# Ten sums and remainders go from VectorE to GpSimd and two come back; token sums and weight splits are issued at other places

## The chip, the cores and the metric

One Trainium2 chip, of which the kernel uses one core. The metric is the device time of one execution in microseconds, the median of the runs. Five engines work side by side, each through its own queue in order, and wait for one another by semaphores: TensorE (PE; its weight loads are PEld), VectorE (DVE), ScalarE (ACT), GpSimd (POOL) and SyncE (SP), which here only issues transfers.

## The reference

One encoder block over 1024 tokens of width 1024, float32, cut to its steps:

```python
h = rms_norm(x, norm1_g)
a, gate, q, k, v = split(h @ w_in)
conv_out = conformer_conv(a, gate, ...)            # gated, 31 taps in depth, norm, silu
attn_out = neighbourhood_attention(q, k, v, rpb)   # 8 heads, 8 x 16 windows
x = x + concat([conv_out, attn_out]) @ w_out
h = rms_norm(x, norm2_g)
x = x + (silu(h @ w_gate) * (h @ w_up)) @ w_down   # width 2816 in between
```

## The kernel before

Every product is made from split operands: a float32 matrix becomes a high part (`hi`, a cast by ScalarE) and a remainder (`lo`, the matrix less its high part, a subtraction by VectorE or GpSimd), and `mac` (L115 to L117) issues three matmuls, hi by hi, hi by lo and lo by hi. The helper `split` (L107 cast, L111 subtraction) takes the engine of the subtraction as an argument.

The feed-forward part works on the transposed state `xT[0..7]` (eight blocks of 128 rows by 1024 tokens) and on pairs i = 0 to 21 of column blocks of the gate and up weights. For each pair the two by two block product (halves of the rows, halves of the tokens) is made with seven products instead of eight, named m1 to m7 as in Strassen's and Winograd's scheme. This needs sums on both sides. On the side of the tokens: S1 to S4 and A22, made in place in `xT` by VectorE (`left`, sums on L1189), each of four blocks k = 0 to 3, with their casts and remainders (L111, or L1196 where the cast was issued apart). On the side of the weights: sums n = 1 to 4 for each pair (`t_sums`, L1024, tile `ts`, or `tqa` for pairs 0 and 1), and the splits of the operands for m1 to m7 (`prep`; tiles `t0m4` and the like, `tqb` and `tqc` for m1 and m2 of pairs 0 and 1, 2 and 3). The results go to the PSUM tiles A (m1, m2), D (m7, m4) and B (m6, m5, m3), and are read out by `evac` and `gate2`: `g` on L1283, L1287 and L1288, `u` on L1274, D on L1259, `g` on L1263. From pair 4 on, m1 and m2 are themselves made from seven smaller products (`part`, tiles `q40m1`, `q41m1`, `q42m1`); for these `tok_sum(m, n)` makes half-width sums of `xT` blocks (L1101, tiles `qtm`) and `prep_part` sums and splits of weights (`qs`, `qa` to `qd`).

Before the feed-forward part stands the output projection (`proj`, PSUM tiles `pj`, weights `wo`, split when `take()` is called), with the residual sum `resid` (L870), which reads `pj`, writes `xT` and frees the PSUM bank for the next `pj`. Then the squares of `xT` are summed (L980) for the second norm, which scales `xT` (`norm2`, L997, with the row `rw` in PSUM).

Nothing schedules the program: each engine's order is the order in which the code issues. The products are issued in the order of the list `products`; behind product number n the entries of the table `after[n]` are issued, then the splits that are due (`prep`). TensorE's order of products around the change is: m1 of pairs 0 and 1, m2 of both, the same for pairs 2 and 3, then m7, m4, m6, m5, m3 for pairs 0 and 1 in turn, then pair 2.

Of the kernel before, what the change touches and what calls it, by code (L numbers as in the profile page):

```python
# [9 lines left out]
OP = mybir.AluOpType  # L10
# [60 lines left out]
def build(ctx, tc, a):  # L71
    nc = tc.nc
    pe, act, dve, pool = nc.tensor, nc.scalar, nc.vector, nc.gpsimd
# [8 lines left out]
    def G(name, dt=F32):  # L82
        return T("G", [P, 1024], 21, name, dt)
# [4 lines left out]
    def H(name, dt=F32):  # L88
        return T("H", [P, 4096], 7, name, dt)
# [16 lines left out]
    def split(hi, lo, src, sub=(pool,)):  # L106
        act.copy(hi, src)  # L107
        n = src.shape[-1] // len(sub)
        for i, eng in enumerate(sub):
            sl = slice(i * n, (i + 1) * n)  # L110
            eng.tensor_tensor(*[w[..., sl] for w in (lo, src, hi.bitcast(F32))], OP.subtract)  # L111
# [7 lines left out]
    def lr(w):  # L119
        return w[:, :512], w[:, 512:]  # L120
# [19 lines left out]
    def issue():  # L140
        if pos[0] < len(chunks):
            src, name, _, _ = chunks[pos[0]]
            if pos[0] not in raws:
                raws[pos[0]] = R(name + "r")
            d = raws[pos[0]]
            if len(src.shape) == 3:
                d = d.rearrange("p (k m) -> p k m", k=src.shape[1])
            sl = slice(512 if name == "wk0" else 0, None)
            nc.sync.dma_start(d[:, sl], src[:, sl])
            pos[0] += 1  # L150

    def take(n=1, ahead=True):
        for _ in range(n):
            i = pos[1]
            while pos[0] <= i:
                issue()
            _, _, dst, sub = chunks[i]
            hi, lo = dst()
            split(hi, lo, raws.pop(i), sub)
            pos[1] += 1  # L160
            if ahead and pos[0] < i + 4:
                issue()
# [650 lines left out]
    def proj(m, h, ks, sel=None, every=1):  # L813
        out = cols(acc[m, h], sel)
        for n, k in enumerate(ks):
            r = [cols(w[:, k % 4], sel) for w in (cm if k < 4 else at)[h]]
            mac(out, [w[:, m % 4 * P:m % 4 * P + P] for w in wo[m // 4, k]], r, k == 4 and sel != INNER, k == 3)
            if n % every == every - 1:
                weave()
# [48 lines left out]
    def resid(m, h):  # L868
        w = xT[m][:, h * 512:(h + 1) * 512]
        dve.tensor_tensor(w, acc[m, h], w, OP.add)  # L870
        nc.sync.dma_start(xd[m][:, h * 512:(h + 1) * 512], w)
# [86 lines left out]
    for k in CONV:  # L958
        for m in range(4):
            proj(m, 0, (k,), None, 1 + (m + 1) % 2)  # L960
            if (k, m) == (3, 0):
                resid(0, 0)
        if k in (1, 2):
            take()
    for m in range(4, 8):
        load_xT(m)
    for m in range(1, 3):
# [31 lines left out]
    HK, QF = KB // 2, FB // 2  # L999
    raw_gu, top, tsum = {}, {}, {}  # L1000

    def load_gu(i, j):
        if i < FB:
            raw_gu[i, j] = R(f"gu{i}{j}")
            nc.sync.dma_start(raw_gu[i, j], a["gu"][ms[i], j])
# [3 lines left out]
    def tq_slot(name, q, dt=F32):  # L1009
        if name not in tqs:  # L1010
            tqs[name] = H(name, dt)
        return tqs[name][:, q * 1024:(q + 1) * 1024]

    def t_sums(i, ns):
        (b11, b21), (b12, b22) = lr(raw_gu[i, 0]), lr(raw_gu[i, 1])
        for n in ns:
            if n in (1, 3):
                if i > 1:
                    tsum[i, n // 2] = G(f"ts{i}{n}")
                else:  # L1020
                    tsum[i, n // 2] = tq_slot("tqa", 2 * i + n // 2)
            o = lr(tsum[i, (n - 1) // 2])[(n - 1) % 2]
            l, r = ((b12, b11), (b22, lr(tsum[i, 0])[0]), (b22, b12), (b21, lr(tsum[i, 0])[1]))[n - 1]
            dve.tensor_tensor(o, l, r, OP.subtract)  # L1024


    ORDER = ("m1", "m6", "m7", "m2", "m5", "m4", "m3")
# [65 lines left out]
    def tok_sum(m, n):  # L1093
        g, c = TOK_AT[n]
        if (m, g) not in tok_raw:
            tok_raw[m, g] = G(f"qt{m}{g}").rearrange("p (c k s) -> p c k s", c=2, s=256)
        for k in range(2):
            x11, x12, x21, x22 = [xT[2 * q + k + HK * (m == "m2")][:, e:e + 256] for q in range(2) for e in (0, 256)]
            s1, s2 = [tok_raw[m, TOK_AT[w][0]][:, TOK_AT[w][1], k] if (m, TOK_AT[w][0]) in tok_raw else None for w in (1, 2)]
            l, r = {1: (x12, x11), 3: (x22, x12), 2: (x22, s1), 4: (x21, s2)}[n]  # L1100
            dve.tensor_tensor(tok_raw[m, g][:, c, k], l, r, OP.subtract)  # L1101
# [49 lines left out]
    def prep(n=1, upto=None):  # L1151
        while tasks and (n > 0 if upto is None else tasks[0][0] <= upto):
            n -= 1
            job = tasks.pop(0)[1]
            if len(job) == 3:
                prep_part(*job)
                continue
            i, p = job
            if i > 1 and p in ("m6", "m7"):
                t_sums(i, (1, 2) if p == "m6" else (3, 4))  # L1160
            b = {"m1": (0, 0), "m2": (0, 1), "m3": (1, 1)}.get(p)
            m = {"m5": 0, "m6": 1, "m7": 2, "m4": 3}.get(p)
            src = lr(raw_gu[i, b[0]])[b[1]] if b else lr(tsum[i, m // 2])[m % 2]
            if i < 4 and p in ("m1", "m2"):
                top[i, p] = lr(tq_slot(("tqb", "tqc")[i // 2], i % 2 + 2 * (p == "m2"), F32R))
            else:
                top[i, p] = lr(G(f"t{i}{p}", F32R))
            split(*top[i, p], src, (dve,) if i < 2 else (pool,))
            if p == ("m7" if i in (2, 3) or parted(i, "m2") else "m2"):
                load_gu(i + 2, 0)  # L1170
            if p == "m3":
                load_gu(i + 2, 1)
# [5 lines left out]
    def block(r, k):  # L1178
        return xT[k % HK + HK * (r[1] == "2")][:, 512 * (r[0] == "2"):512 * (r[0] == "2") + 512]

    def left(n, k, what, sub=dve):
        if n not in sop:
            q = H(n, F32R).rearrange("p (w k s) -> p w k s", w=2, s=512)
            sop[n] = [[q[:, h, i] for i in range(HK)] for h in range(2)]
        o, l, r, op = {"S3": ("21", "11", "21", OP.subtract), "A22": ("22", "22", "22", None),
                       "S2": ("22", "22", "21", OP.subtract), "S1": ("21", "22", "11", OP.add),
                       "S4": ("22", "12", "22", OP.subtract)}[n]
        if op is not None and "sum" in what:
            dve.tensor_tensor(block(o, k), block(l, k), block(r, k), op)  # L1189
        hi, lo = sop[n][0][k], sop[n][1][k]  # L1190
        if "split" in what:
            split(hi, lo, block(o, k), (sub,))
        if "cast" in what:
            act.copy(hi, block(o, k))
        if what == "sub":
            sub.tensor_tensor(lo, block(o, k), hi.bitcast(F32), OP.subtract)  # L1196

    def lefts(n, sub=(dve,) * 4, first=None, upto=HK):
        for k in range(HK + 1):
            if k < HK:  # L1200
                first(k) if first else left(n, k, "sum")
            if 0 < k <= upto:
                left(n, k - 1, "split", sub[k - 1])

    def h2_one(k):
        norm2(k, 0)
# [6 lines left out]
    for m in range(4):  # L1213
        square(m, 0)
    beside = {(1, 1): [lambda: token_sums(0)], (1, 3): [lambda: token_rows(0)],
              (0, 1): [lambda: t_sums(0, (1, 2))], (0, 3): [lambda: t_sums(0, (3, 4))],
              (2, 1): [lambda: t_sums(1, (1, 2))], (3, 1): [lambda: t_sums(1, (3, 4))]}
    for kb, at_ in enumerate(((2, 0), (2, 3), (2, 6), (3, 1), (3, 4), (3, 7), (4, 3), (4, 7))):
        beside.setdefault(at_, []).append(lambda kb=kb: h2_one(kb))
# [162 lines left out]
    def prep_items(n):  # L1382
        for _ in range(n):
# [8 lines left out]
             6: lambda: [left("S1", k, "sum cast") for k in range(HK)],  # L1392
             7: lambda: left("S1", 0, "sub"),
             8: lambda: [left("S1", k, "sub") for k in (1, 2)],
             9: lambda: (left("S1", 3, "sub"), prep(), [tok_sum("m1", w) for w in (1, 3)]),
             10: lambda: ([tok_sum("m1", w) for w in (2, 4)], prep(), [left("S4", k, "sum cast") for k in range(HK)]),
             11: lambda: [left("S4", k, "sub") for k in (0, 1)],
             12: lambda: ([left("S4", k, "sub") for k in (2, 3)], prep()),
             18: lambda: [tok_sum("m2", w) for w in (1, 3)],
             19: lambda: [tok_sum("m2", w) for w in (2, 4)]}  # L1400
    prep(4)
# [46 lines left out]
    def quarter(w, o, t):  # L1448
        return w[:, o + t * 512:o + t * 512 + 512]
# [32 lines left out]
    for s, p in enumerate(SEQ):  # L1482
        for k in range(QF - 2):
            n = s * QF + k
# [23 lines left out]
    for half in range(2):  # L1508
# [4 lines left out]
        w = quarter(om["u"], 0, 3)[:, part_]  # L1513
# [17 lines left out]
```

## Time and profile before

| | |
|---|---|
| median of 3 runs | 1035.74 us (1035.32 to 1035.88) |
| profiled execution | 1035.18 us |
| its span | 1033.5 us |
| busy share of the span | PE 99%, PEld 83%, DVE 76%, ACT 46%, POOL 42% |
| granted TensorE clock | 1.0 throughout |
| transfers | 152.53 MB, mean 148 GB/s |

How to read it: the profile is one execution, and every share is an average over stages with different limits. Matmuls overlap, so that TensorE's busy share says little about short losses; these are read from the starts of successive matmuls. The chain that ended last gives 93% to PE and 5% to DVE; in the timeline of that chain the DVE part lies mostly between 415 and 475 us, where the first products of the feed-forward part are made. Names in profile rows leave out buffer numbers, so `S` may be any of S1 to S4, and `D<-A` is a product of A22 into D.

### The profile page before, as it was taken

The page shows a single profiled execution, that of the slowest core. Times are in us where ns is not written, and L with a number is a line of the kernel's source. Part 1 is how long each engine was busy: PE and PEld are TensorE (multiplying, and loading weights), DVE is VectorE, ACT ScalarE, POOL GpSimd, SP SyncE. Part 2 cuts the span into 40 slices and gives each one's busy share as a digit, 9 for nine tenths or more (in the row PEclk, how much of TensorE's full clock was granted, in tenths as well). Part 3 has the DMA queues.
Part 4 walks back from the last instruction along what each step waited for, and adds up shares of the span by engine and source line. Part 5 has one row for each costly group of instructions (what it writes and reads, how often), then busy time and mean ns, then how long its engine had stood idle before and what let it go on. Part 6 is the DMA issues. An engine that isn't in the chain of part 4 may idle for free.

```text
span 1033.5 us, 15158 instructions
## 1 busy us (share of the span) xinstructions
PE 1024.3 (99%) x5334; PEld 853.8 (83%) x5334; DVE 782.3 (76%) x1234; ACT 478.7 (46%) x1045; POOL 436.0 (42%) x345
## 2 busy tenths in 40 slices
PE   9999999999999999999999999999999999999998
PEld 7888888877787788877888888888888888888887
DVE  5788997896755376998787787787787767758874
ACT  7565348836866345523334334343342443433432
POOL 1036764524641345047776667567566200003210
PEclk9999999999999999999999999999999999999999
DMA  9426781337403621122434424434441696633631
GB/s 347 165 79 201 225 255 53 122 115 234 124 22 122 235 92 41 47 107 89 156 119 157 139 96 153 153 101 145 144 143 71 222 365 238 224 102 123 214 122 42
DMA packets 75084, 152.53 MB, mean 148 GB/s; under 512 B 13824, under 2 KB 22784, under 8 KB 74368
## 3 DMA queue, kind: packets, MB, share of 16 engines
q1 hardware_dynamic: 72992, 148.21, 42.5%
q10 hardware_dynamic: 2016, 3.36, 0.9%
q8 instruction: 42, 0.69, 0.3%
q14 instruction: 34, 0.28, 0.1%
HBM read 112.38 MB, written 44.76 MB: 152 GB/s over the span
## 4 chain that ended last, share of the span: by engine, by line
PE 93%; DVE 5%; ACT 1%; issue 1%; DMA 0%; ACTq 0%; DVEq 0%
PE B L115 5%; PE B L116 5%; PE B L117 5%; PE z L115 4%; PE z L117 4%; PE z L116 4%; PE D L115 3%; PE D L116 3%; PE D L117 3%; PE gl L117 3%; PE gl L116 3%; PE gl L115 3%; PE pj L115 3%; PE pj L116 3%; PE pj L117 3%; PE p L720 2%
## 5 line engine op out<-in xcount | busy, mean ns | idle before, releaser
L363 DVE SCALAR_TENSOR_TENSOR cv<-u,par,cv 128x1009 f32<-128x1009 f32 (+14 forms) x92 | 117.4, 1277 | 2.3
L389 POOL TENSOR_TENSOR pa<-pa,pr 128x1022 f32<-128x1022 f32 (+5 forms) x24 | 58.0, 2417 | 48.7 <-ACT pr L388 36.1
L107 ACT CAST op<-sr 128x512 fp32r<-128x512 f32 x77 | 47.7, 619 | 57.7 <-PE B2d L117 26.7
L1474 POOL TENSOR_TENSOR ou<-ou,resm 128x512 f32<-128x512 f32 x8 | 12.0, 1506 | 139.8 <-DVE ou L1465 126.1
L111 DVE TENSOR_TENSOR op<-sr,op 128x512 fp32r<-128x512 f32 x77 | 57.6, 748 | 16.5 <-ACT op L107 16.4
L709 POOL TENSOR_SCALAR e<-e,rs 128x288 f32<-128x288 f32 (+1 forms) x64 | 33.9, 545 | 41.8 <-DVE rs L707 40.1
L1024 DVE TENSOR_TENSOR ts<-gu,ts 128x512 f32<-128x512 f32 x40 | 46.3, 1158 | 0.7
L107 ACT CAST op<-wd 128x512 fp32r<-128x512 f32 x54 | 33.4, 619 | 28.5 <-DVE wd L1370 18.0
L698 ACT ACTIVATE e<-e,mx 128x288 f32<-128x288 f32 (+1 forms) x64 | 36.5, 572 | 18.8 <-DVE mx L693 16.9
L111 DVE TENSOR_TENSOR op<-wd,op 128x512 fp32r<-128x512 f32 x54 | 39.8, 738 | 1.7 <-ACT op L107 0.6
L693 DVE CUSTOM_DVE_ANT_0 e<-s,tab 128x288 f32<-128x288 f32 (+1 forms) x64 | 28.7, 503 | 13.6 <-PE s L680 13.6
L980 POOL TENSOR_TENSOR sq<-sq,sq 128x512 f32<-128x512 f32 x12 | 17.1, 1423 | 51.6 <-ACT sq L976 51.4
L1283 DVE TENSOR_TENSOR g<-D,g 128x512 f32<-128x512 f32 x22 | 15.2, 690 | 23.4 <-PE D L117 23.4
L416 ACT ACTIVATE sq<-z,r 128x64 f32<-128x64 f32 x96 | 28.3, 329 | 5.2 <-PE z L117 5.2
L1260 ACT ACTIVATE D<-D 128x512 f32<-128x512 f32 x22 | 12.8, 582 | 32.6 <-DVE D L1259 32.6
L388 ACT ACTIVATE pr<-u,par 128x1022 f32<-128x1022 f32 (+5 forms) x24 | 27.0, 1138 | 1.6 <-ACT vs L446 1.2
L720 PEld LDWEIGHTS p<-ident,e 128*96 128x96 f32 (+1 forms) x192 | 20.5, 133 | 6.8 <-POOL e L709 6.3
L115 PE MATMUL B2d<-op 128*128 128x512 f32 x66 | 25.8, 391 | 0.0
L117 PE MATMUL B2d<-op 128*128 128x512 f32 x66 | 25.7, 389 | 0.0
L116 PE MATMUL B2d<-op 128*128 128x512 f32 x66 | 25.7, 389 | 0.0
L739 PE MATMUL o<-e,vw 96*64 96x128 f32 (+1 forms) x384 | 24.7, 277 | 0.0
L720 PE MATMUL p<-ident,e 128*96 128x128 f32 (+1 forms) x192 | 24.4, 276 | 0.0
(1454 smaller groups left out, 3734.5 us busy)
## 6 DMA issues: line engine op xcount, KB each, us to landing
gu<-in_gu SPq DMA_DIRECT2D x44, 512.0 KB
sr<-sd SPq DMA_DIRECT2D x77, 256.0 KB
sd<-sd SPq DMA_DIRECT2D x22, 512.0 KB
wd<-in_wd SPq DMA_DIRECT2D x36, 256.0 KB
sd<-g SPq DMA_DIRECT2D x33, 256.0 KB
x<-in_x SPq DMA_DIRECT2D x8, 512.0 KB
xT<-in_xp SPq DMA_DIRECT2D x8, 512.0 KB
xd<-xT SPq DMA_DIRECT2D x16, 256.0 KB
```

Source lines behind the costliest of these rows:

```text
L107: act.copy(hi, src)
L111: eng.tensor_tensor(*[w[..., sl] for w in (lo, src, hi.bitcast(F32))], OP.subtract)
L115: pe.matmul(acc, lh, rh, start=start, stop=False, skip_group_check=True)
L116: pe.matmul(acc, lh, rl, start=False, stop=False, skip_group_check=True)
L117: pe.matmul(acc, ll, rh, start=False, stop=stop, skip_group_check=True)
L363: dve.scalar_tensor_tensor(acc[:, o], uc[:, i], dwk[:, c, t:t + 1], acc[:, o], OP.mult, OP.add)
L389: pool.tensor_tensor(pa[:, o], pa[:, o], pr[:, o], OP.add)
L693: dve.tensor_tensor_reduce(out=es[i][:, hh], in0=s[hh], in1=tab[rh, cb][2 * hp + hh], scale=-1.0, scalar=3.0e38, op0=OP.add, op1=OP.min, a ...
L698: act.activation(e, e, AF.Exp, bias=mx.pop((i, hh)), scale=-1.0, accum_out=sums[i][:, hh:hh + 1])
L709: pool.tensor_scalar(es[i][:, hh], es[i][:, hh], rs[:, hh:hh + 1], 1.0, op0=OP.mult, op1=OP.mult)
L720: pe.transpose(pt[:m, g * P:(g + 1) * P], es[i][:, hh, g * m:(g + 1) * m], ident)
L1024: dve.tensor_tensor(o, l, r, OP.subtract)
```

## The change

Ten subtractions named in a set `ON_POOL` are issued on GpSimd instead of VectorE: the remainders of S3 (k = 2, 3), A22 (k = 1) and S4 (k = 3), the weight sums n = 2 and 4 of pair 3, and the remainders of the weight operands m4 and m5 of pair 0 and m4 and m6 of pair 1. Two, the remainders of m3 and m7 of pair 3 (`ON_DVE`), go the other way. The split of the weights wo16, issued by the second of two `take()` calls, moves behind the residual sum of block 0. Of the token sums of m1, each two half-width subtractions, n = 2 moves one product earlier, n = 3 three later and n = 4 five later.

```diff
             proj(m, 0, (k,), None, 1 + (m + 1) % 2)
             if (k, m) == (3, 0):
                 resid(0, 0)
-        if k in (1, 2):
-            take()
+            if (k, m) in ((1, 3), (3, 0)):
+                take()
...
+    ON_POOL = {("S3", 2), ("S3", 3), ("A22", 1), ("S4", 3), (3, 2), (3, 4),
+               (0, "m4"), (0, "m5"), (1, "m4"), (1, "m6")}
+    ON_DVE = {(3, "m3"), (3, "m7")}
...
-            dve.tensor_tensor(o, l, r, OP.subtract)
+            (pool if (i, n) in ON_POOL else dve).tensor_tensor(o, l, r, OP.subtract)
...
-            split(*top[i, p], src, (dve,) if i < 2 else (pool,))
+            on_dve = (i < 2 and (i, p) not in ON_POOL) or (i, p) in ON_DVE
+            split(*top[i, p], src, (dve,) if on_dve else (pool,))
...
-    def left(n, k, what, sub=dve):
+    def left(n, k, what):
+        sub = pool if (n, k) in ON_POOL else dve
...
-             9: lambda: (left("S1", 3, "sub"), prep(), [tok_sum("m1", w) for w in (1, 3)]),
-             10: lambda: ([tok_sum("m1", w) for w in (2, 4)], prep(), [left("S4", k, "sum cast") for k in range(HK)]),
+             9: lambda: (left("S1", 3, "sub"), prep(), [tok_sum("m1", w) for w in (1, 2)]),
+             10: lambda: (prep(), [left("S4", k, "sum cast") for k in range(HK)]),
              11: lambda: [left("S4", k, "sub") for k in (0, 1)],
-             12: lambda: ([left("S4", k, "sub") for k in (2, 3)], prep()),
+             12: lambda: ([left("S4", k, "sub") for k in (2, 3)], prep(), tok_sum("m1", 3)),
+             15: lambda: tok_sum("m1", 4),
```

The orders of TensorE, ScalarE and SyncE are the same in both programs; those of VectorE and GpSimd differ in the places named. VectorE at the end of the output projection, where the residual sum of block 0 (L870, `xT0`) and the split of wo16 stand; first the program before, then the one after:

```order
L111 TENSOR_TENSOR cm1_3173<-z12_3503,cm1_3173 128x512
L111 TENSOR_TENSOR wo14_3480<-wo16r_3266,wo14_3480 128x1024
L870 TENSOR_TENSOR xT0_3416<-pj00_3088,xT0_3416 128x512
L111 TENSOR_TENSOR cm1_3173<-z13_3521,cm1_3173 128x512
L111 TENSOR_TENSOR wo10l_3544<-wo10r_3268,wo10h_3543 128x1024
```

```order
L111 TENSOR_TENSOR cm1_3173<-z12_3503,cm1_3173 128x512
L870 TENSOR_TENSOR xT0_3416<-pj00_3088,xT0_3416 128x512
L111 TENSOR_TENSOR wo14_3480<-wo16r_3266,wo14_3480 128x1024
L111 TENSOR_TENSOR cm1_3173<-z13_3521,cm1_3173 128x512
L111 TENSOR_TENSOR wo10l_3544<-wo10r_3268,wo10h_3543 128x1024
```

The two rows of `xT0` and `wo16r` have changed places (the tile `wo14` holds wo16's parts too).

VectorE between the sums of S3 and of S2, where the norms (L997) of blocks 4 to 7 and the remainders of S3 and A22 stand; before, then after:

```order
L1189 TENSOR_TENSOR xT3_3422<-xT3_3422 128x512
L111 TENSOR_TENSOR S3_4054<-xT2_3420,S3_4054 128x512
L111 TENSOR_TENSOR S3_4054<-xT3_3422,S3_4054 128x512
L997 SCALAR_TENSOR_TENSOR xT4_3535<-xT4_3535,par_73,rw1_4042 128x512
L997 SCALAR_TENSOR_TENSOR xT5_3537<-xT5_3537,par_73,rw1_4042 128x512
L111 TENSOR_TENSOR A22_4112<-xT4_3535,A22_4112 128x512
L997 SCALAR_TENSOR_TENSOR xT6_3539<-xT6_3539,par_73,rw1_4042 128x512
L111 TENSOR_TENSOR A22_4112<-xT5_3537,A22_4112 128x512
L997 SCALAR_TENSOR_TENSOR xT7_3541<-xT7_3541,par_73,rw1_4042 128x512
L111 TENSOR_TENSOR A22_4112<-xT6_3539,A22_4112 128x512
```

```order
L1195 TENSOR_TENSOR xT3_3422<-xT3_3422 128x512
L997 SCALAR_TENSOR_TENSOR xT4_3535<-xT4_3535,par_73,rw1_4042 128x512
L997 SCALAR_TENSOR_TENSOR xT5_3537<-xT5_3537,par_73,rw1_4042 128x512
L111 TENSOR_TENSOR A22_4112<-xT4_3535,A22_4112 128x512
L997 SCALAR_TENSOR_TENSOR xT6_3539<-xT6_3539,par_73,rw1_4042 128x512
L997 SCALAR_TENSOR_TENSOR xT7_3541<-xT7_3541,par_73,rw1_4042 128x512
L111 TENSOR_TENSOR A22_4112<-xT6_3539,A22_4112 128x512
```

S3's last two remainders and A22's second are gone from VectorE; they stand on GpSimd behind the `tqc` splits.

GpSimd between the split of `qb4m1` and that of `qc4m1`, which TensorE's parts `q41m1` and `q42m1` use (`ts31` and `ts33` hold the weight sums of pair 3, `qT3m1` a token sum); before, then after:

```order
L111 TENSOR_TENSOR qb4m1_4456<-qs4m1_4451,qb4m1_4456 128x512
L111 TENSOR_TENSOR t3m6_4462<-ts31_4459,t3m6_4462 128x512
L111 TENSOR_TENSOR qT3m1_4465<-qtm10_4225,qT3m1_4465 128x512
L111 TENSOR_TENSOR t3m7_4485<-ts33_4482,t3m7_4485 128x512
L111 TENSOR_TENSOR qc4m1_4521<-qs4m1_4451,qc4m1_4521 128x512
```

```order
L111 TENSOR_TENSOR qb4m1_4456<-qs4m1_4451,qb4m1_4456 128x512
L1028 TENSOR_TENSOR ts31_4459<-gu31_4246,ts31_4459 128x512
L111 TENSOR_TENSOR t3m6_4462<-ts31_4459,t3m6_4462 128x512
L111 TENSOR_TENSOR qT3m1_4465<-qtm10_4225,qT3m1_4465 128x512
L1028 TENSOR_TENSOR ts33_4482<-gu30_3802,ts31_4459 128x512
L111 TENSOR_TENSOR qc4m1_4521<-qs4m1_4451,qc4m1_4521 128x512
```

Two sums have come in, and the split of `t3m7` has gone to VectorE, where it stands behind the sum n = 3.

More of the change, by code (lines that the diff above doesn't have):

```diff
@@ L1196, in left, with lefts @@
             sub.tensor_tensor(lo, block(o, k), hi.bitcast(F32), OP.subtract)
-    def lefts(n, sub=(dve,) * 4, first=None, upto=HK):
+    def lefts(n, first=None, upto=HK):
         for k in range(HK + 1):
@@ L1202, in lefts @@
             if 0 < k <= upto:
-                left(n, k - 1, "split", sub[k - 1])
+                left(n, k - 1, "split")
     def h2_one(k):
```

## The prediction

> **What bounds the kernel now.** I read the page first, then the list of who waited for whom on TensorE, then the timeline of TensorE around each of these waits, then the timelines of VectorE (DVE), ScalarE (ACT) and GpSimd (POOL) over the same stretch. The page and one row of the table by stage:
>
> ```profile
> span 1033.5 us, 15158 instructions
> ...
> PE 1024.3 (99%) x5334; PEld 853.8 (83%) x5334; DVE 782.3 (76%) x1234; ACT 478.7 (46%) x1045; POOL 436.0 (42%) x345
> ```
>
> ```profile
> 430.00:440.00 10.00, 10.00 (x45) 8.25 (x45) 10.00 (x21) 3.18 (x6) 0.00 (x0) 1.00 0.45 150
> ```
>
> TensorE is idle for 1033.5 - 1024.3 = 9.2 us in all, so nothing off TensorE can bring more than some 1%. But in the stretch of the first products VectorE is the full engine: from 430 to 440 us it is busy 10.00 of 10.00 us, ScalarE 3.18, GpSimd 0.00. What a late VectorE costs there shows in TensorE's timeline, at five places (start, duration, and in brackets the idle time and who ended it):
>
> ```profile
> 337.51 0.40 PE L117 MATMUL pj<-cm,wo02l 128*128 128x512 f32 x1
> 338.96 0.50 PE L115 MATMUL pj<-at,wo 128*128 128x512 f32 x1 [1.05 <-DVE xT L870]
> ...
> 428.73 0.39 PE L116 MATMUL D<-S,t1m 128*128 128x512 f32 x1
> 428.95 0.39 PE L117 MATMUL D<-S,t1m 128*128 128x512 f32 x1
> 429.78 0.50 PE L115 MATMUL D<-A,t0m 128*128 128x512 f32 x1 [0.43 <-DVE g L1283]
> ...
> 443.29 0.39 PE L117 MATMUL B<-S,t0m 128*128 128x512 f32 x1
> 444.13 0.50 PE L115 MATMUL B<-S,t1m 128*128 128x512 f32 x1 [0.46 <-DVE u L1274]
> 444.47 0.40 PE L116 MATMUL B<-S,t1m 128*128 128x512 f32 x1
> ...
> 446.80 0.39 PE L117 MATMUL B<-S,t1m 128*128 128x512 f32 x1
> 447.45 0.47 PE L115 MATMUL B<-S,t0m 128*128 128x512 f32 x1 [0.26 <-ACT t2m L107]
> ...
> 465.78 0.28 PE L116 MATMUL q41m<-qT2m,qb4m 128*128 128x256 f32 x1
> 465.89 0.28 PE L117 MATMUL q41m<-qT2m,qb4m 128*128 128x256 f32 x1
> 466.58 0.49 PE L115 MATMUL B<-S,t2m 128*128 128x512 f32 x1 [0.41 <-DVE g L1283]
> ```
>
> Matmuls overlap, so the loss is read from start to start. Those of 512 columns follow at 0.22 to 0.23 us (428.73, 428.95; 0.227 below), those of 256 columns at 0.11 to 0.12. After a wait the next matmul comes 0.34 behind (444.13 to 444.47), which is 0.11 more. So the five places lose: P1 (338.96) 1.45 - 0.23 + 0.11 = 1.33; P2 (429.78) 0.83 - 0.23 = 0.60, the 0.11 left aside; P3 (444.13) 0.84 - 0.23 + 0.11 = 0.72; P4 (447.45) 0.65 - 0.23 + 0.11 = 0.53; P5 (466.58) 0.69 - 0.12 + 0.11 = 0.68. Together 3.86 us. TensorE's order isn't changed, so these are what can be won.
>
> **The change, part by part.** All times below are in the clock of the profile before; what is won at one place moves everything behind it forward together.
>
> *P1, the two weight splits.* TensorE waits for the residual sum L870 of block 0, which frees the PSUM bank:
>
> ```profile
> 336.13 0.69 DVE L111 TENSOR_TENSOR cm<-z,cm 128x512 fp32r<-128x512 f32 x1 [0.74 <-ACT cm L107]
> 337.08 1.23 DVE L111 TENSOR_TENSOR wo<-wo16r,wo 128x1024 fp32r<-128x1024 f32 x1 [0.26 <-ACT wo L107]
> 338.22 0.68 DVE L870 TENSOR_TENSOR xT<-pj,xT 128x512 f32<-128x512 f32 x1
> 338.82 0.68 DVE L111 TENSOR_TENSOR cm<-z,cm 128x512 fp32r<-128x512 f32 x1
> ```
>
> The sum stands behind the split of wo16, and is moved ahead of it. VectorE operations of 512 columns follow each other at 0.60 us (338.22 to 338.82), so it can start at 336.13 + 0.60 = 336.73 and ends at 337.41, before TensorE's next slot at 337.74: P1 goes, with 0.3 us to spare. Late next are the splits: wo16's now starts at 337.33 and ends at 338.56, against 339.1 for its first matmul (six matmuls behind 337.74). The ones of wo10 and wo12, in unchanged order, end only about 0.1 us earlier than before while TensorE comes 1.33 earlier; by this reckoning the last meets its matmul with nothing to spare, so I keep 0 to 0.3 us of loss there for the range and take 0. Transfers and ScalarE's order are the same. Gain 1.33.
>
> *P2, three of four remainders of S3 and A22 to GpSimd.* TensorE waits there for g L1283, which stands in VectorE's queue behind them:
>
> ```profile
> 416.95 0.69 DVE L111 TENSOR_TENSOR A<-xT,A 128x512 fp32r<-128x512 f32 x1
> ...
> 418.22 0.68 DVE L111 TENSOR_TENSOR A<-xT,A 128x512 fp32r<-128x512 f32 x1
> ...
> 429.04 0.68 DVE L1283 TENSOR_TENSOR g<-D,g 128x512 f32<-128x512 f32 x1
> ```
>
> ```profile
> 416.30 1.23 ACT L107 CAST A<-xT 128x512 fp32r<-128x512 f32 x2
> 418.33 0.62 ACT L107 CAST A<-xT 128x512 fp32r<-128x512 f32 x1 [0.81 <-DVE xT L997]
> ```
>
> The two of S3 stand ahead of 416.95 and free 2 x 0.60, but the operation at 416.95 needs ScalarE's first cast of A22 (416.30 to 416.92), so these 1.2 us turn into idle time. The one at 418.22 is A22's second; without it the next norm and all behind it come 0.60 earlier, and g ends at 429.72 - 0.60 = 429.12. TensorE's slot is 428.95 + 0.23 = 429.18: P2 goes, just. Gain 0.60; ends 0 and 0.71.
>
> *P3 and P4, the token sums and the fourth remainder (S4).*
>
> ```profile
> 433.98 1.42 DVE L1101 TENSOR_TENSOR qtm<-xT,qtm 128x256 f32<-128x256 f32 x4
> ...
> 443.39 0.68 DVE L1274 TENSOR_TENSOR u<-B,g 128x512 f32<-128x512 f32 x1
> ...
> 446.63 0.68 DVE L1283 TENSOR_TENSOR g<-B,g 128x512 f32<-128x512 f32 x1
> ```
>
> Of eight half-width sums (four in 1.42, 0.34 each) ahead of u at 443.39 four go, two come back between, and the S4 remainder goes: u starts at 443.39 - 0.60 (from P2) - 1.36 + 0.68 - 0.60 = 441.5 and ends at 442.2. TensorE's slot is 443.52 - 0.60 = 442.9: P3 goes, with 0.7 to spare. At P4 the row names a cast of t2m, but the bank that TensorE overwrites is freed by g at 446.63, which ends at 447.31; I take g, and the cast waits for VectorE's sums in the same queue. g stands 3.24 behind u: 444.8, ending 445.4. TensorE's slot, 447.03 less P2 and P3, is 445.7: P4 goes, with 0.3 to spare. The last two sums return in a stretch where VectorE waits for TensorE anyway. Gain 1.25; ends 0.6 and 1.25.
>
> *P5, the two weight sums of pair 3 to GpSimd, two splits back.*
>
> ```profile
> 464.27 1.65 DVE L1024 TENSOR_TENSOR ts<-gu,ts 128x512 f32<-128x512 f32 x1
> 465.85 0.68 DVE L1283 TENSOR_TENSOR g<-B,g 128x512 f32<-128x512 f32 x1
> ```
>
> ```profile
> 463.70 1.68 POOL L111 TENSOR_TENSOR qb4m<-qs4m,qb4m 128x512 fp32r<-128x512 f32 x1 [5.62 <-ACT qb4m L107]
> ...
> 472.63 1.30 POOL L111 TENSOR_TENSOR qc4m<-qs4m,qc4m 128x512 fp32r<-128x512 f32 x1 [0.96 <-ACT qc4m L107]
> ```
>
> The sum at 464.27 leaves; g starts there instead of 465.85 and ends 1.0 us ahead of TensorE's slot at 466.01. Gain 0.68. On GpSimd both sums now stand ahead of qc4m, for which TensorE's q42m waits. qb4m ends at 465.38; four operations (two sums, two splits) and one cast on ScalarE of 0.7 follow, at 1.30 to 1.68 each: qc4m can start between 471.3 and 472.8, plus 0.68 since P5 moves TensorE but not GpSimd: 472.0 to 473.5, against 472.63. Loss 0 to 0.9; I take 0.25, near the middle. The t3m7 split that comes back to VectorE (0.60, and a wait for its cast, with D L1259 and the rest of gate and up queued behind it) uses the 1.58 that the sum at 464.27 set free.
>
> *Four weight remainders of pairs 0 and 1 to GpSimd.* No wait of TensorE stands near them. They are queued ahead of the token-square sums L980 and of the tqc splits:
>
> ```profile
> 395.24 1.29 POOL L980 TENSOR_TENSOR sq<-sq,sq 128x512 f32<-128x512 f32 x1 [2.02 <-ACT sq L976]
> 399.15 1.30 POOL L980 TENSOR_TENSOR sq<-sq,sq 128x512 f32<-128x512 f32 x1 [2.62 <-ACT sq L976]
> 403.51 5.09 POOL L111 TENSOR_TENSOR tqc<-gu,tqc 128x512 fp32r<-128x512 f32 x4 [3.06 <-ACT tqc L107]
> ```
>
> ```profile
> 412.86 0.39 PE L115 MATMUL A<-h,tqc 128*128 128x512 f32 x1
> ```
>
> They need 4 x 1.30 = 5.2, and GpSimd idles 2.02 + 2.62 + 3.06 = 7.7 there; the splits end at 408.6, the matmuls need them at 412.86. Nothing; if that cover were gone, each microsecond over 4 would cost one.
>
> *The sum.* 1.33 + 0.60 + 1.25 + 0.68 - 0.25 = 3.6 us. The profiled execution took 1035.18 (span 1033.5 and 1.7 around it), which gives 1031.6; the median of the three runs, 1035.74, lies 0.56 above it, which gives 1032.1. I forecast 1032.1.
>
> **What GpSimd does to VectorE meanwhile.** Two pairs of rows:
>
> ```profile
> 387.00 1.74 POOL L980 TENSOR_TENSOR sq<-sq,sq 128x512 f32<-128x512 f32 x1
> ...
> 453.60 1.30 POOL L111 TENSOR_TENSOR qT1m<-qtm,qT1m 128x512 fp32r<-128x512 f32 x1
> ```
>
> ```profile
> 387.51 1.39 DVE L997 SCALAR_TENSOR_TENSOR xT<-xT,par,rw 128x512 f32<-128x512 f32 x2
> ...
> 453.91 1.54 DVE L1288 TENSOR_TENSOR g<-sl,g 128x512 f32<-128x512 f32 x1
> ```
>
> The VectorE operation at 453.91 has both inputs in SBUF. It starts inside a GpSimd operation (453.60 to 454.90) and takes 1.54 instead of 0.68, ending 0.55 after the other. The norms at 387.51 read one input from PSUM; they run beside GpSimd at full pace, two in 1.39. The Trainium skill, SBUF — State Buffer, section "Who interferes with whom", says that a VectorE instruction with two SBUF inputs and a GpSimd instruction that reads SBUF exclude each other, the second waiting for the whole of the first. By that rule the trace agrees, and it speaks against this change: the moved operations could stop VectorE for longer than they took on it. Met in full by each of the four that leave VectorE's fullest stretch, it gives the time of the first rival below instead of the sum above.
>
> **The rivals.** *Slower: GpSimd stops VectorE.* Each of the four operations moved out of 411 to 441 us frees 0.60 of VectorE and holds it up for x. With x = 1.74 (the GpSimd row at 387.00) VectorE's queue grows by 4 x 1.14 = 4.6; P2 to P4 ride on that queue, so the kernel loses 4.6 - 1.33 = 3.2: 1038.9. It decides from x = 0.93 (no change), and is slower by 0.2% from x = 1.45. For it: the pair at 453. Against it: beside S3's two and A22's one VectorE has norms, which read PSUM, and the wait for the cast until 416.92; beside S4's it has u and D, which read PSUM. I reckon x at 0 to 0.3. Chance 0.06.
>
> *ScalarE holds VectorE.* If what is freed turns into waits for casts, as with S3's 1.2 us, P2 to P4 stay: 1.33 + 0.68 - 0.25 = 1.8, so 1034.0. Against it: VectorE's 10.00 of 10.00 and ScalarE's 3.18 from 430 on. Chance 0.12.
>
> *It doesn't do what it says.* Semaphores are shared, so TensorE could be held by another operation that ends as late: 1035.7. Against it: each of the five waits ends within 0.15 us of the operation named. Chance 0.04.
>
> **How the numbers follow.** The forecast holds 0.78. Its own range: down to a gain of 2.3 (0.3 lost at P1, 0.6 at P2 or at P3 and P4, 0.4 more at q42m), 1033.4; up by 0.25 if q42m loses nothing, 0.56 if the base is the profile's own time, and 0.9 for the rest of TensorE's 9.2 us of idle time, which I did not price: 1030.4. The range reaches on to the ScalarE case: 1030.4 to 1034.3; outside lie the other two rivals and some edge. A difference of 0.2%, 2.1 us, is about what a measurement of this kernel can tell from no change; faster means below 1033.7. Faster: 0.78 and half of the 0.12, 0.84. Same: the other half, the last rival, and a little of the first (x between 0.93 and 1.45), 0.11. Slower: what is left of the first, 0.05.
>
> **What would show it.** In the profile after: no wait of TensorE for xT L870 with pj<-at at about 337.7; D<-A some 0.6 nearer to its predecessor; no gap at the two B<-S places; g at P5 right behind the first sum, with q42m waiting for qc4m a little longer; VectorE operations on two SBUF inputs not longer than 1 us between 411 and 441. Wrong it is if those last, or if the gap ahead of D<-A grows.

## The result, and the profile after

The changed kernel took 1031.07 us in the median of six runs (1030.59 to 1031.57), the kernel before 1035.76 in six beside it (1035.23 to 1035.88): 4.69 us less, a ratio of 0.9956 with a 95% interval of 0.9945 to 0.9968. A second comparison on another occasion gave 1031.45 against 1035.47, 4.02 us less, 0.9958 (0.9945 to 0.9972). The forecast was 1032.1, a gain of 3.6.

The page of the changed kernel, its span, the busy time of the engines, and the chain that ended last:

```profile
span 1028.9 us, 15157 instructions
...
PE 1022.9 (99%) x5334; PEld 854.4 (83%) x5334; DVE 771.8 (75%) x1226; ACT 479.4 (47%) x1045; POOL 447.7 (44%) x353
...
PE 96%; DVE 2%; ACT 1%; POOL 1%; issue 0%; POOLq 0%; ACTq 0%; DVEq 0%
```

TensorE's idle time falls from 9.2 to 1028.9 - 1022.9 = 6.0 us, VectorE's share of the chain from 5% to 2%. VectorE is busy 10.5 us less: the ten operations that left took 11.4 there, five of them 1.4 to 1.8 each beside an operation of GpSimd, and the two that came take 2.0; the remaining 1.1 was not followed up. GpSimd is busy 11.7 more. This is the list of the waits of TensorE after (time in all, times, longest):

```profile
PE up L274 <- POOL ones L270: 1.0, 1, 1.0
PE q41m L117 <- POOL qb4m L111: 0.5, 1, 0.5
PE D L115 <- DVE g L1269: 0.4, 1, 0.4
PE s L680 <- DVE e L727: 0.3, 1, 0.3
PE pj L116 <- DVE cm L111: 0.2, 1, 0.2
```

None of the five waits of the prediction is left (line numbers have moved: u L1274 is L1280 now, g L1283 is L1289). TensorE's timeline at the five places, each with the matmul ahead of it:

```profile
337.18 0.40 PE L117 MATMUL pj<-cm,wo02l 128*128 128x512 f32 x1
337.41 0.39 PE L115 MATMUL pj<-at,wo 128*128 128x512 f32 x1
...
427.27 0.39 PE L117 MATMUL D<-S,t1m 128*128 128x512 f32 x1
427.50 0.47 PE L115 MATMUL D<-A,t0m 128*128 128x512 f32 x1
...
440.98 0.39 PE L117 MATMUL B<-S,t0m 128*128 128x512 f32 x1
441.20 0.39 PE L115 MATMUL B<-S,t1m 128*128 128x512 f32 x1
...
443.69 0.39 PE L117 MATMUL B<-S,t1m 128*128 128x512 f32 x1
443.92 0.39 PE L115 MATMUL B<-S,t0m 128*128 128x512 f32 x1
...
462.28 0.28 PE L117 MATMUL q41m<-qT2m,qb4m 128*128 128x256 f32 x1
462.40 0.40 PE L115 MATMUL B<-S,t2m 128*128 128x512 f32 x1
```

Each step is the plain one, 0.22 to 0.23 us, and 0.12 behind the half-width product. The table by stage shows what became of VectorE (columns: stretch, length; busy time and number on PE, PEld, DVE, ACT, POOL; clock, transfer share, GB/s):

```profile
420.00:430.00 10.00, 10.00 (x45) 8.12 (x44) 9.91 (x17) 5.67 (x10) 0.00 (x0) 1.00 0.00 0
430.00:440.00 10.00, 10.00 (x46) 8.29 (x45) 9.93 (x20) 4.19 (x7) 1.56 (x1) 1.00 0.34 111
```

VectorE is still full from 420 to 440: what left was not replaced by idle time, its queue only runs ahead of TensorE now. Neither sign of being wrong that the prediction named is there: D<-A follows at the plain step, and of VectorE's operations that start between 411 and 441 us none takes over 0.74.

**How the runs are read below.** TensorE's order is the same in all kernels, so each matmul can be set against the same matmul of the profile before. The table gives what each place wins: the difference of the starts ahead of the place (median of the nine matmuls before it) less the one behind it (median of eight). The last column is the difference (less than zero: earlier than before) that is there ahead of P1, where no kernel here differs from another.

| kernel (label) | P1 | P2 | P3 | P4 | P5 | ahead of P1 |
|---|---|---|---|---|---|---|
| forecast | 1.33 | 0.60 | 0.72 | 0.53 | 0.68 | |
| changed kernel | 1.34 | 0.64 | 0.77 | 0.54 | 0.69 | -0.34 |
| the same again (after2) | 1.34 | 0.64 | 0.77 | 0.54 | 0.69 | +0.65 |
| a_resid | 1.32 | 0.01 | 0.01 | -0.04 | 0.00 | +0.44 |
| b_lefts | 0.00 | 0.64 | 0.62 | -0.03 | 0.00 | +0.35 |
| c_tokens | 0.00 | 0.01 | 0.61 | 0.53 | 0.00 | +0.47 |
| d_sums3 | 0.00 | -0.02 | 0.06 | -0.01 | 0.69 | -0.14 |
| g_s3only | 0.00 | 0.02 | 0.01 | -0.02 | 0.00 | +0.20 |
| e_w01 | 0.00 | -0.05 | 0.03 | -0.01 | 0.00 | +0.30 |
| f_s2two | 1.34 | -0.01 | 0.77 | 0.54 | 0.69 | +0.10 |
| f_s2 | 1.34 | -1.02 | 0.77 | 0.54 | 0.69 | +0.27 |

The last column shows why parts of a microsecond are read by place and not by the times alone: two profiles of the changed kernel differ by 0.99 us ahead of P1, and by as much already at 10 us, in the first products. The table covers only the five places; what is won and lost between them is said with the experiments.

### The profile page after: what moved, and what is told of

It reads as the page before. It is cut to its first block, busy times and chain, and to the rows that moved or that the text cites. A ratio compares the mean times of both kernels' runs of the same rounds, so it can differ in the third digit from the quotient of the medians.

```text
span 1028.9 us, 15157 instructions
## 1 busy us (share of the span) xinstructions
PE 1022.9 (99%) x5334; PEld 854.4 (83%) x5334; DVE 771.8 (75%) x1226; ACT 479.4 (47%) x1045; POOL 447.7 (44%) x353
## 4 chain that ended last, share of the span: by engine, by line
PE 96%; DVE 2%; ACT 1%; POOL 1%; issue 0%; POOLq 0%; ACTq 0%; DVEq 0%
PE B L116 5%; PE B L115 5%; PE B L117 5%; PE z L115 4%; PE z L117 4%; PE z L116 4%; PE D L115 4%; PE D L116 4%; PE D L117 4%; PE gl L115 3%; PE gl L116 3%; PE gl L117 3%; PE pj L116 3%; PE pj L115 3%; PE pj L117 3%; PE p L720 2%
## 5 line engine op out<-in xcount | busy, mean ns | idle before, releaser
L1028 DVE TENSOR_TENSOR ts<-gu,ts 128x512 f32<-128x512 f32 x38 | 42.8, 1127 | 0.7
L1289 DVE TENSOR_TENSOR g<-D,g 128x512 f32<-128x512 f32 x22 | 15.2, 690 | 23.1 <-PE D L117 23.1
L870 DVE TENSOR_TENSOR xT<-pj,xT 128x512 f32<-128x512 f32 x16 | 10.8, 687 | 19.1 <-PE pj L117 18.8
```

The source lines that it names most:

```text
L1028: (pool if (i, n) in ON_POOL else dve).tensor_tensor(o, l, r, OP.subtract)
```

## Experiments: one part of the change alone

Each of these is the kernel before with one part of the change. The times of the first four are medians beside the kernel before (1035.69 in 33 runs).

**The weight split alone (a_resid).**

```diff
-        if k in (1, 2):
-            take()
+            if (k, m) in ((1, 3), (3, 0)):
+                take()
```

> Only the wo16 split moves behind the residual sum of block 0; everything else as before. My theory: the wait at P1 (1.33 us from start to start) goes whole and nothing comes back behind it, so 1.0 to 1.33 us less than the kernel before, TensorE's start offset 1.33 at all later places, and the waits at P2 to P5 as before. Rival, the split as the next late one: the gain is given back at wo16's or wo12's first matmul, a new wait of up to 1.2 us for a split of wo, 0 to 0.3 us less. Rival, doesn't do what it says: the bank is freed by another operation, 0.

Measured: 1034.41, 1.28 us less, ratio 0.9988 (0.9979 to 0.9996). TensorE's timeline:

```profile
337.95 0.39 PE L117 MATMUL pj<-cm,wo02l 128*128 128x512 f32 x1
338.18 0.40 PE L115 MATMUL pj<-at,wo 128*128 128x512 f32 x1
...
342.75 0.50 PE L117 MATMUL pj<-cm,wo12l 128*128 128x512 f32 x1
```

P1 goes whole and P2 to P5 stand. But 0.15 us comes back at the splits: VectorE ends the remainder of wo12 at 342.70, the first matmul that uses it starts at 342.75, and the next one follows 0.34 behind (343.09) instead of 0.23. In the changed kernel 0.15 to 0.2 is lost at the same matmul. So the first expectation holds in its size, 1.32 - 0.15 = 1.2 us by place, but not in that nothing comes back; the first rival named the right place, with far too large a loss. The second rival falls.

**The four token remainders alone (b_lefts).**

```diff
+    ON_POOL = {("S3", 2), ("S3", 3), ("A22", 1), ("S4", 3)}
```

> Only the four token remainders (S3 k = 2, 3; A22 k = 1; S4 k = 3) go to GpSimd; all else as before. My theory: P2 goes (0.60), P3 goes (u two operations earlier, 0.72), P4 goes in part (0 to 0.2, g then ends 0.4 after TensorE's slot), P1 and P5 stay: 1.2 to 1.5 us less than before. The port rival (each moved operation holds VectorE for 1.74): VectorE's queue grows by 4.6, 3 to 4.6 us more than before, with VectorE rows on two SBUF inputs of over 1 us between 411 and 441. The ScalarE rival: freed time becomes waits for casts, P2 to P4 stay, 0 us.

Measured: 1034.09, 1.60 us less, 0.9983 (0.9974 to 0.9992). P2 goes, P3 goes but for some 0.1 (0.62), P4 stays whole; by place that is 1.23 us, within the 1.2 to 1.5 expected. The port rival, 3 to 4.6 us slower, and the ScalarE rival, no gain, are both out for this set. That P4 stays, where I had left it 0 to 0.2, is taken up below.

**The token sums alone (c_tokens).**

```diff
-             9: lambda: (left("S1", 3, "sub"), prep(), [tok_sum("m1", w) for w in (1, 3)]),
-             10: lambda: ([tok_sum("m1", w) for w in (2, 4)], prep(), [left("S4", k, "sum cast") for k in range(HK)]),
+             9: lambda: (left("S1", 3, "sub"), prep(), [tok_sum("m1", w) for w in (1, 2)]),
+             10: lambda: (prep(), [left("S4", k, "sum cast") for k in range(HK)]),
...
+             12: lambda: (..., tok_sum("m1", 3)),
+             15: lambda: tok_sum("m1", 4),
```

> Only the token sums of m1 move (n = 2 one product earlier, n = 3 three later, n = 4 five later); nothing goes to GpSimd. My theory: u starts 0.68 earlier, so P3 goes (0.72), P4 goes in part (0.2), P1, P2 and P5 stay: 0.7 to 1.2 us less than before. The ScalarE rival: u waits for something else, P3 and P4 stay, 0 us. If the sums that come back (n = 3, 4) meet a wait of TensorE between 447 and 466: less than 0.7, with a new wait there.

Measured: 1034.40, 1.29 us less, 0.9988 (0.9979 to 0.9997). P3 goes but for some 0.1 (0.61) and, unlike in the run above, P4 goes whole, where 0.2 of it was expected; the time is just outside the 0.7 to 1.2 expected, the 1.14 by place inside. The half-width sums between 447 and 466 cost TensorE nothing.

Why P4 goes here and not in b_lefts is in the timelines of VectorE and GpSimd. In the kernel before, and in b_lefts, the weight sum between u and the g that frees the bank takes twice its time (two rows of before, then two of b_lefts):

```profile
444.72 1.38 DVE L1024 TENSOR_TENSOR ts<-gu 128x512 f32<-128x512 f32 x1
...
444.26 1.29 POOL L111 TENSOR_TENSOR t2m<-ts,t2m 128x512 fp32r<-128x512 f32 x1 [35.66 <-ACT t2m L107]
```

```profile
443.81 1.38 DVE L1027 TENSOR_TENSOR ts<-gu 128x512 f32<-128x512 f32 x1
...
443.36 1.28 POOL L111 TENSOR_TENSOR t2m<-ts,t2m 128x512 fp32r<-128x512 f32 x1 [2.88 <-ACT t2m L107]
```

In c_tokens:

```profile
444.55 0.71 DVE L1027 TENSOR_TENSOR ts<-gu 128x512 f32<-128x512 f32 x1
...
443.42 1.29 POOL L111 TENSOR_TENSOR t2m<-ts,t2m 128x512 fp32r<-128x512 f32 x1 [34.34 <-ACT t2m L107]
```

In the first two, VectorE's sum has both inputs in SBUF and starts 0.45 us into a GpSimd operation; it ends 0.55 (before: 446.10 against 445.55) behind that operation's end, as in the pair that the prediction showed at 453. In c_tokens the token sum n = 3 stands ahead of u, VectorE reaches the weight sum when GpSimd's operation has 0.16 left, and it takes 0.71. So g comes not 3.24 behind u but 445.78 - 443.22 = 2.56. Part of P4 was a meeting of the two engines that the kernel before already had; the change took it away by moving the token sums. This is read from the rows: without the 0.67, g of b_lefts would end at 445.73, ahead of its slot at 446.08, instead of at 446.40. It was not tried by itself.

**The weight sums of pair 3 alone (d_sums3).**

```diff
+    ON_POOL = {(3, 2), (3, 4)}
+    ON_DVE = {(3, "m3"), (3, "m7")}
```

> Only the two weight sums of pair 3 go to GpSimd and the splits of m3 and m7 of pair 3 to VectorE; all else as before. My theory: P5 goes (0.68) and q42m waits for qc4m on GpSimd 0 to 0.9 us longer, 0.25 taken: 0.4 to 0.7 us less than before. Rival, GpSimd gives all back: qc4m ends as much later as P5 gained, 0, with a wait of q42m of 0.7 or more. Rival, port: VectorE's g beside the sum on GpSimd takes 1.5 instead of 0.68 and P5 stays.

Measured: 1034.81, 0.88 us less, 0.9991 (0.9983 to 1.0). The interval reaches no change, so the times alone say little. By place P5 goes with 0.69, and 0.05 to 0.1 is given back by 480 us, which leaves 0.6, within the 0.4 to 0.7 expected. The term for q42m was 0.25; the loss is smaller and most of it stands elsewhere. The changed kernel's GpSimd and TensorE rows:

```profile
464.21 1.30 POOL L111 TENSOR_TENSOR t3m<-ts,t3m 128x512 fp32r<-128x512 f32 x1 [0.74 <-ACT t3m L107]
467.17 1.30 POOL L1028 TENSOR_TENSOR ts<-gu,ts 128x512 f32<-128x512 f32 x1
468.43 1.29 POOL L111 TENSOR_TENSOR qc4m<-qs4m,qc4m 128x512 fp32r<-128x512 f32 x1
...
465.58 0.47 PE L117 MATMUL B<-S,t3m 128*128 128x512 f32 x1
465.89 0.40 PE L115 MATMUL B<-S,t3m 128*128 128x512 f32 x1
469.50 0.28 PE L116 MATMUL q42m<-qT3m,qc4m 128*128 128x256 f32 x1
469.77 0.39 PE L117 MATMUL q42m<-qT3m,qc4m 128*128 128x256 f32 x1
```

Before, GpSimd idled 0.96 ahead of qc4m, waiting for its cast; now the second sum fills that time and qc4m follows at once. It starts 472.63 - 468.43 = 4.20 earlier than before, where TensorE runs 4.2 to 4.3 earlier. q42m's third matmul, the first that uses qc4m's remainder, comes 0.28 behind its second. But it came 0.24 behind it in the kernel before too (473.75 to 473.99), so only 0.04 is new, and 0.02 in d_sums3. The larger loss is at m6 of pair 3: its operand now waits for the first moved sum, and its remainder ends on GpSimd at 465.51. The matmul at 465.58 that uses it is followed 0.31 behind instead of 0.23, 0.08 lost. The prediction had no term for this.

**Two parts without effect at the five places (g_s3only, e_w01).**

```diff
+    ON_POOL = {("S3", 2), ("S3", 3)}                            # g_s3only
+    ON_POOL = {(0, "m4"), (0, "m5"), (1, "m4"), (1, "m6")}      # e_w01
```

> Only the two remainders of S3 (k = 2, 3) go to GpSimd; all else as before. My theory: the 1.2 us that they free on VectorE become idle time ahead of A22's first remainder, which waits for ScalarE's cast; P2 to P5 stay as before and TensorE's starts do not move: 0 us. If this wait were not the limit there, P2 would go with 0.60 and P3 with up to 0.72. The port rival: the rows of VectorE beside them are longer, and P2 grows by up to 1.1.

> Only the four weight remainders of pairs 0 and 1 (m4, m5; m4, m6) go to GpSimd; all else as before. My theory: no place of TensorE's moves, 0 us, and GpSimd's tqc splits end before the matmuls that use them. Rival, GpSimd late: a new wait of TensorE for tqc near 412, up to 1.2 us. Port rival: VectorE's two-input rows beside them grow, and P2 grows with them.

Measured in one execution each: 1035.40 and 1035.18 (the kernel before beside them 1035.73), and none of the five places moves by more than 0.05. VectorE's timeline in g_s3only:

```profile
417.10 0.69 DVE L111 TENSOR_TENSOR A<-xT,A 128x512 fp32r<-128x512 f32 x1 [1.50 <-ACT A L107]
```

The freed 1.2 us stand as idle time ahead of A22's first remainder. So S3's two bring nothing, and for them the ScalarE rival was right.

In e_w01 TensorE's starts do move, by 0.2 us, ahead of P2. The sums of squares for the norm (`ss`, L985) waited a little in the kernel before (first row) and no longer do in e_w01 (second):

```profile
403.86 1.02 PE L985 MATMUL ss<-one,sq 128*128 128x1 f32 x8
```

```profile
404.03 0.95 PE L985 MATMUL ss<-one,sq 128*128 128x1 f32 x8
```

The step from the matmul ahead is 0.35 before (403.51 to 403.86) and 0.23 in e_w01 (403.80 to 404.03), and the second `ss` matmul comes 0.08 closer behind the first. Before, the last residual sum (401.52) followed two weight remainders on VectorE; in e_w01 it waits for TensorE instead. The changed kernel wins the same 0.2. The wait is too short for the list, so the expectation of 0 us missed it.

As b_lefts won P2 and P3 with S3's two on board, P2 is A22's second remainder and P3 the S4 one behind it (neither was run by itself).

## Experiments: does GpSimd stop VectorE?

**Two and four more remainders, beside sums that read SBUF (f_s2two, f_s2).** S2's remainders go to GpSimd as well, where VectorE makes the sums of S2 and S1 (L1195).

```diff
-    ON_POOL = {("S3", 2), ("S3", 3), ("A22", 1), ("S4", 3), ...
+    ON_POOL = {("S3", 2), ("S3", 3), ("A22", 1), ("S4", 3), ("S2", 0), ("S2", 1), ...                          # f_s2two
+    ON_POOL = {("S3", 2), ("S3", 3), ("A22", 1), ("S4", 3), ("S2", 0), ("S2", 1), ("S2", 2), ("S2", 3), ...    # f_s2
```

> The changed kernel, and the four remainders of S2 go to GpSimd as well, where VectorE has the sums L1195 with both inputs in SBUF beside them (in the changed kernel the moved remainders stand beside operations that read PSUM, or beside idle time). If GpSimd and VectorE exclude each other when both read SBUF: VectorE rows L1195 of 1.2 to 2 us instead of 0.68 between 417 and 427, a wait of TensorE of 1 to 2 us ahead of D<-A (427.50), 1 to 2.5 us slower than the changed kernel. If they do not: the four free another 2.4 us of VectorE, no wait, 0 against the changed kernel.

> The changed kernel, and two remainders of S2 (k = 0, 1) on GpSimd instead of all four. If each that meets a two-input sum L1195 costs VectorE some 1.1 us and frees 0.60: VectorE is 1.0 later, of which P2 has 0.3 to spare, so a wait ahead of D<-A with 0.5 to 1.0 us lost, and two stretched sums. If there is no exclusion, 0; if the cost of all four was a late GpSimd rather than a late VectorE, 0 too.

Measured: f_s2 1033.12 (0.9977 of the kernel before, 0.9968 to 0.9987), against 0.9956 and 0.9958 for the changed kernel on other occasions; f_s2two 1031.63 against 1031.45 for the changed kernel beside it, which by the times alone is no difference. By place: f_s2 loses 0.64 + 1.02 = 1.66 us at P2 against the changed kernel, f_s2two 0.65, both within what was expected. In f_s2two only one of the sums is stretched, not two; the other time is lost on a remainder of VectorE's own behind them. The instructions of L1195 with two inputs (number; shortest, median and longest in ns), in the changed kernel, in f_s2two and in f_s2; then GpSimd's remainders of S2 in f_s2:

```profile
L1195 DVE TENSOR_TENSOR xT<-xT,xT x8: 684/685/686, 418.5 to 425.5; 128x512 f32<-128x512 f32 x8
```

```profile
L1195 DVE TENSOR_TENSOR xT<-xT,xT x8: 676/680/1786, 418.9 to 426.6; 128x512 f32<-128x512 f32 x8
...
428.49 0.50 PE L115 MATMUL D<-A,t0m 128*128 128x512 f32 x1 [0.44 <-DVE g L1289]
```

```profile
L1195 DVE TENSOR_TENSOR xT<-xT,xT x8: 680/1232/1791, 419.1 to 427.8; 128x512 f32<-128x512 f32 x8
...
L111 POOL TENSOR_TENSOR S<-xT,S x4: 1629/1740/1743, 420.5 to 425.5; 128x512 fp32r<-128x512 f32 x4
...
PE D L115 <- DVE g L1289: 1.5, 1, 1.5
```

The longest sum takes 1.79 instead of 0.68: 1.11 us. In f_s2 the eight sums, one behind the other, take 9.32 us from the first start to the last end, 4.4 more than at 0.60 each: 1.1 us for each of the four remainders, which free 0.60 each. So VectorE falls back by 4 x 0.5 = 2.0, of which 1.66 reach TensorE. GpSimd's operations grow too, from 1.30 to 1.74. The rule of the Trainium skill, SBUF — State Buffer, section "Who interferes with whom", which the prediction weighed, agrees with these rows: operations on two SBUF inputs and GpSimd's take turns.

In the numbers of the slower rival, x is 1.1 here, above the 0.93 from which it decides (1.04 if P5 and q42m, which that sum left out, are counted): the mechanism is real, and the forecast came out because the change does not bring it about where it moves work. Beside S3's two remainders and A22's, in the changed kernel, stand idle time and norms, which read PSUM:

```profile
412.63 2.54 POOL L111 TENSOR_TENSOR S<-xT,S 128x512 fp32r<-128x512 f32 x2 [6.46 <-ACT S L107]
415.87 1.31 POOL L111 TENSOR_TENSOR A<-xT,A 128x512 fp32r<-128x512 f32 x1 [0.70 <-ACT A L107]
435.56 1.56 POOL L1202 TENSOR_TENSOR S<-xT,S 128x512 fp32r<-128x512 f32 x1 [18.39 <-ACT S L1200]
...
412.32 1.40 DVE L997 SCALAR_TENSOR_TENSOR xT<-xT,par,rw 128x512 f32<-128x512 f32 x2
415.24 0.69 DVE L111 TENSOR_TENSOR A<-xT,A 128x512 fp32r<-128x512 f32 x1 [1.52 <-ACT A L107]
415.85 1.40 DVE L997 SCALAR_TENSOR_TENSOR xT<-xT,par,rw 128x512 f32<-128x512 f32 x2
```

Two norms take 1.40 beside GpSimd, and 1.40 in the kernel before at 415.47, where GpSimd stands idle. S4's remainder came while VectorE was at a remainder of its own; there GpSimd paid (1.56 instead of 1.30).

**One more token sum later (k_n3).** Meant to bring the meeting at P4 back.

```diff
-             12: lambda: ([left("S4", k, "sub") for k in (2, 3)], prep(), tok_sum("m1", 3)),
-             15: lambda: tok_sum("m1", 4),
+             12: lambda: ([left("S4", k, "sub") for k in (2, 3)], prep()),
+             15: lambda: [tok_sum("m1", w) for w in (3, 4)],
```

> The changed kernel with the token sums n = 3 also moved to the place of n = 4, so that two half-width sums (0.67 us) leave VectorE's queue ahead of the second u. By the count of the queue alone, u and the g behind it (442.46) both come 0.67 earlier. By the meeting with GpSimd: u comes 0.67 earlier (439.2), but the weight sum that follows then starts inside GpSimd's remainder of t2 (440.10 to 441.39) and takes 1.38 instead of 0.71, and g stays within 0.1 of 442.46. TensorE's starts are the same as in the changed kernel in both cases.

Measured in one execution: 1032.81, 1.4 us above the changed kernel beside it. Neither expectation holds for TensorE. The rows: VectorE's weight sum and the two half-width sums that were moved, then GpSimd's remainder, then TensorE:

```profile
442.13 0.69 DVE L1028 TENSOR_TENSOR ts<-gu 128x512 f32<-128x512 f32 x1 [0.76 <-PE B L117]
...
446.25 1.20 DVE L1105 TENSOR_TENSOR qtm<-xT,xT 128x256 f32<-128x256 f32 x2
...
440.82 1.29 POOL L111 TENSOR_TENSOR t2m<-ts,t2m 128x512 fp32r<-128x512 f32 x1 [2.94 <-ACT t2m L107]
...
458.77 0.47 PE L115 MATMUL D<-A,t2m 128*128 128x512 f32 x1 [0.36 <-DVE g L1289]
...
463.81 0.39 PE L117 MATMUL q41m<-qT2m,qb4m 128*128 128x256 f32 x1 [1.12 <-POOL qb4m L111]
```

The weight sum waited for a product of TensorE until GpSimd's operation was over (442.11), so they did not meet, and the run does not test the reading of P4. What it shows is the price of a place: the two half-width sums take 1.20 where they now stand, instead of 0.76 in the changed kernel, VectorE runs late from there on, and TensorE loses 0.6 to 0.7 us against the changed kernel at each of two waits. That they grow by meeting GpSimd is my reading of the row and was not tried by itself.

## A version that beats both

The changed kernel's list of waits names two more of this kind. h_both issues the remainder of qb4 (for m1 of pair 4) on VectorE, where it takes 0.69 us instead of 1.69, and the last g of a pair (L1269) ahead of the read-out of m3:

```diff
-            split(*quad[j, 1], sum4[j][:, :512], (pool,))
+            split(*quad[j, 1], sum4[j][:, :512], (dve,) if j == ("m1", 4) else (pool,))
...
     for n, (i, p) in enumerate(products):
         ...
         pacc = product(i, p)
+        if late and p == "m3":
+            late.pop(0)()
         evac(i, p, pacc)
```

> The changed kernel with two more steps, aimed at the two waits of TensorE that are left between 455 and 475: the remainder of qb4 for m1 of pair 4 goes from GpSimd to VectorE, and the last g of a pair (L1269) is issued ahead of the read-out of m3 instead of behind it. My theory (waits of this kind are won from start to start): 0.5 us at q41m (461.82) and 0.4 at D<-S (470.93), so 0.7 to 0.9 us less than the changed kernel, 4.6 to 5.6 less than before. Rival: the waits come back later at the next operation of VectorE's queue, 0 to 0.3.

> The changed kernel with the two more steps (remainder of qb4 on VectorE, L1269 ahead of the read-out of m3) once more, beside the changed kernel on the same chip: 0.9 to 1.2 us less than it by TensorE's starts from 160 us to 480 us, 0.5 to 1.2 by the medians.

Measured: 1030.31 and, beside the changed kernel, 1030.36 against 1031.45; ratio to the kernel before 0.995 (0.9938 to 0.9963) and 0.995 (0.9937 to 0.9962). The waits of TensorE in the first of the two:

```profile
PE up L274 <- POOL ones L270: 1.0, 1, 1.0
PE s L680 <- DVE e L727: 0.3, 1, 0.3
PE pj L116 <- DVE cm L111: 0.2, 1, 0.2
PE B L115 <- DVE g L1289: 0.2, 1, 0.2
```

Both waits are gone and a small one is new: g at P5 now stands behind the remainder of qb4. From ahead of P1 to 480 us the starts win 1.2 us on the changed kernel, more than the 0.7 to 0.9 expected of the first run. That expectation added the idle times of the list, 0.5 and 0.4. Read from start to start, as for P1 to P5, the two waits of the changed kernel cost 0.74 (461.07 to 461.82) and 0.68 (470.24 to 470.93), and the new one costs 0.43. Behind 480 us both runs win 0.2 more near 530 and lose 0.3 near 821, which leaves 1.0 to 1.1 at the last matmul; these two were not followed up.

## Why the prediction was right, and where it was off

- **P1 to P5.** Forecast 3.86 us, measured 3.98, none off by more than 0.05. The step that carried it, reading each wait from start to start with the 0.11 behind it, holds for P1, P4 and P5 one by one in a_resid, c_tokens and d_sums3; P3 goes whole only when both of its parts are in. P2's 0.11, left aside, came in part (0.64).
- **S3's two remainders and the weights of pairs 0 and 1** were costed at nothing, by the wait for ScalarE's cast and by the lack of a waiting TensorE: g_s3only shows the first. The second was nearly right: no listed wait stands there, but e_w01 wins 0.2 at the sums of squares.
- **P1's splits.** The working let wo12's remainder meet its matmul with nothing to spare, kept 0 to 0.3 for the range and took 0; 0.15 to 0.2 is lost there.
- **P4.** The gain was right; the working was incomplete. I carried the 3.24 from u to g over unchanged, and 0.67 of it was a meeting with GpSimd that went away. In the changed kernel that only adds to the spare time: g ends at 443.14, 0.78 ahead of its slot, where I had 0.3. By the rows of b_lefts and c_tokens it decides P4 there.
- **q42m, 0.25,** is the term that was mis-sized: 0.02 to 0.04, and 0.08 more is lost at m6 of pair 3, for which there was no term. I counted four operations and a cast by bounds, and took the middle, although the row showed 0.96 us of GpSimd's idle time just ahead of qc4m.
- **The rest.** By place, 3.98 - 0.2 (wo12) + 0.2 (sums of squares) - 0.1 (m6 and q42m) = 3.9 us come from the change. That the first two cancel is luck. In the profile of the first comparison TensorE's last start comes 4.18 earlier, of which 0.34 is there ahead of P1, and the stretch behind it is 0.35 shorter; that stretch takes 3.5 to 4.0 in the profiles here, and what sets it was not looked into. So 4.69 holds parts that aren't the five places'; the second comparison, 4.02, is nearer to 3.9.
- **The rivals.** GpSimd's stop is real at 1.1 us for a meeting, but at another place; ScalarE held two of the four remainders; what the five places gave came each from the part that the prediction named.

## What to carry to other kernels

An operation that leaves a full engine pays only if what stands behind it there was next for the engine that waits: of ten moved operations three stood ahead of such a wait (A22's second, S4's last, the first weight sum of pair 3), S3's two brought nothing, and the four weight remainders 0.2 us at a wait too short for the list (the second weight sum was not tried alone). Before work goes from VectorE to GpSimd, look at what VectorE does beside it: next to operations that read PSUM or next to idle time it cost nothing, next to sums on two SBUF inputs it cost 1.1 us for the 0.60 that it freed. When a wait is gone, read the list again: two more, of 0.4 and 0.5 us of idle time, stood there, and moving two operations won another 1.1 us. And where a start to start step looks like a new wait, look at the same step in the kernel before: of the 0.16 at q42m 0.12 had been there.

## What was not expected of the hardware

- A meeting costs both sides: VectorE's sum 0.68 to 1.79 us, GpSimd's remainder 1.30 to 1.74 (f_s2). Where VectorE was first, GpSimd alone paid: 1.56 (S4's remainder).
- Two profiles of the same program, taken on two occasions, differ by 0.99 us before the first place at which any of these kernels differ, at a granted clock of 1.0 in both. Differences below a microsecond between two single executions are not the change's until the place is shown.
